# Numerators of two attention groups kept in SBUF, mixing factors formed and transposed earlier in a visit, and head 0 of a recurrence tied behind three sums

## The chip, the cores and the metric

The kernel runs on one core of a Trainium2 chip. The metric is the device time of one execution in microseconds, as the median of several runs. TensorE is PE in the profile, VectorE is DVE, ScalarE is ACT, GpSimd is POOL and SyncE is SP. Matrix products write into PSUM banks, of which there are eight; DVE and ACT read them from there. DMA transfers are issued by SP, POOL and ACT.

## The reference

One layer of an encoder for 1024 positions of width 1024, in float32:

```python
proj = x @ w_in          # aq, ak, av: 12 heads x 64; gq, gk: 4 x 64; gv: 4 x 128; gates
for gi, (win, dil) in enumerate(((128, 1), (512, 4), (2048, 16))):   # three groups of 4 heads
    o_g, lse_g = dilated_group(aq, ak, av, bias(gi), dil, win // 2 // dil)
mix_w = softmax(stack(lses), axis=0)
y_attn = sum(mix_w * stack(outs))                       # 1024 x 256
o_gla = gla_forward(...) + flip(gla_backward(...))      # decays by chunk, 4 heads
y_gla = o_gla * rsqrt(mean(o_gla ** 2)) * gla_norm_g * silu(gout)
merged = sigmoid(gate_a) * (y_attn @ wa) + sigmoid(gate_g) * (y_gla @ wg)
x = layernorm(ALPHA * x + merged @ w_out)
x = layernorm(ALPHA * x + square(relu(x @ w_ff1 + b)) @ w_ff2 + b)
```

A query attends keys within a window of its group, at a stride; each group has its own softmax, and the three outputs are mixed with weights that follow from the three softmax denominators. With e = exp(score − m) and den = sum(e) of a group, the mixed output is the sum over groups of exp(m_g − M)·(e_g·v) divided by the sum of exp(m_g − M)·den_g, M being the largest of the three m_g. The kernel calls e_g·v the numerator and exp(m_g − M) divided by that sum the factor.

## The kernel before

A product of two float32 matrices is made of three matmuls on parts: every operand is split into a rounded high part (a copy or cast on ACT) and a remainder (a subtraction on DVE), and `mm3` (L99 to L104) issues high·high, high·low and low·high. The large projections use seven products of half-size blocks in place of eight (Winograd's form of Strassen's scheme), so sums of blocks are formed on DVE ahead of the matmuls and sums of products behind them (`add`, L160). Twelve matmuls of 128x512 are called a step here.

**The order.** A scheduler decides the order of instructions on each engine from its own estimate of time; `tc.issue_after(x)` forbids it to put an instruction ahead of x, and `behind("name")` is that with the last instruction recorded under the name. The dictionary `issued` holds these: "add" is the last sum of products, "pe" the last matmul of a projection or of the recurrence, "small" the last small matmul of attention, "raw" and "sp" the last transfer issued on SP, "pool" the last one on POOL. All engines work in their own order and wait for others by semaphores.

**Head 0 of the recurrence.** At the end of the first projections (`psteps`, ten steps, L724 to L743) PE makes the products of q and k for the recurrence. Each step's result is read by a sum on DVE into `fu` or `fcr` and stored to `spill` in DRAM; the banks are called mm, tr and av. While that goes on, head 0 is prepared: `pre1` makes logarithms of decays, `scan` (L513, L514) sums them by chunk, `pre2` (L520 to L533) subtracts, makes exponentials on ACT, and multiplies k by `ex` and q by `zb` on DVE. `load_qk` brings q and k of heads 0 and 1 back from `spill` by SP: two transfers for each. The pieces `firsts[p]` belong to the next projections: `[0]` issues the load of weights `raw`, `[1]` casts them to `whi` on ACT (L93) and makes `wlo` on DVE (L95). Behind the steps follow `fill(1)` (two steps of the next projections, copied out by ACT at L630 as `xb`), `turn` (transposes k, ACT copies `kt`, L542), `intra` (scores inside a chunk, L581) and `kv` (k transposed times v, L550).

**Attention.** 24 tiles of 128 queries, in the order of group 2, group 1, group 0 (g = 2, 1, 0, eight tiles t each), are worked off between the steps of the projections of gates. `visit(i)` is issued at step `at[i]` and holds parts of several tiles: the loads of tile i+1, the value products of tile i−2 (L941, into the bank `avp`), the scores of tile i (L902, into two banks sc; DVE adds the bias and takes the row minimum, L908, and ACT makes the exponentials), the mixing of tile i−2, the transposes of the exponentials of tile i−1 (L926, into two banks tr; DVE and ACT copy them to `et`), and `spread` of tile i−1. A step later follow `weigh`, `shares`, `loadw` and `store`. For groups 2 and 1 the numerator is copied from `avp` to SBUF (L954), stored to `numdr` in DRAM by POOL, and brought back later by SP in quarters (`quarter`) into the tiles R. For group 0, `weigh` and `shares` (L986 to L1002) form the factors f from the minima and denominators of the three groups, `spread` transposes f on PE (L1008) into the score bank of the newest scores, ACT copies that to `fT` and stores it to `fdr`, `loadw` reads it back, repeated over 64 partitions, into W, and `mix` multiplies numerators by W and adds (L962 to L971). The result goes to `yadr`.

**The gates.** `gate_load` and `gate` bring the outputs of the recurrence and their gates into SBUF, apply silu on ACT, multiply and split on DVE, at fixed steps of the same loop.

The rows at which the profile points are these lines: L102 to L104 matmuls, L160 sums, L95 and L93 splits of weights, L530 and L533 the products with k and q, L542 and L550 `kt` and `kv`, L902, L908, L926, L941, L954, L962, L970, L1002 and L1008 as above.

## Time and profile before

| | |
|---|---|
| median of 3 runs | 1371.03 us (1369.74 to 1373.22) |
| the profiled execution | 1369.64 us, span 1367.9 us, clock of TensorE 0.996 |
| first projections, head 0 | to about 110 us of the span |
| recurrence, with first products of the next projections | 110 to about 340 us |
| attention between projections | 341 us (first value product) to 566 us (last mixing) |
| merge, output projection, norms, feed-forward part | behind about 600 us |
| busy, share of the span | PE 98%, DVE 76%, ACT 47%, POOL 10% |

The waits view names, for an engine and a line, what it waited for, the sum in us, how often, and the longest. A row of a timeline has its start, its duration, the engine, the line, the operation with what it writes and reads, and in brackets how long the engine was idle before it and what ended that. A row of the windows view has the stretch, its length, then the busy time and number of instructions of PE, of PE's weight loads, DVE, ACT and POOL, then the clock that TensorE was granted (1.00 is full), the mean share of the 16 DMA engines, and GB/s.

### The profile page before, as it was taken

To read this page: it belongs to the slowest core of one execution; us is meant where nothing else is said; L and a number is where in the kernel's file an instruction comes from. 1 tells how busy PE (TensorE), PEld (TensorE's weight loads), DVE (VectorE), ACT (ScalarE), POOL (GpSimd) and SP (SyncE) were. 2 spreads that over 40 slices of the span, in tenths; PEclk is the share of its full clock that TensorE was granted. 3 is DMA by queue.
4 is the path that set the end of the run, shared out by engine and by line. 5 is a ranking of instruction groups with operands and counts; after the bars stand their busy time and mean duration, and the time that the engine had idled before them with its cause. 6 is when DMAs were issued, how large, how long until landed. Compare 5 with 4: busy or idle time off the path is not lost.

```text
span 1367.9 us, 19100 instructions
## 1 busy us (share of the span) xinstructions
PE 1346.4 (98%) x6757; PEld 1119.6 (82%) x6757; DVE 1033.7 (76%) x1786; ACT 637.6 (47%) x1200; POOL 143.5 (10%) x228
## 2 busy tenths in 40 slices
PE   9989999999999998999999999999999999999998
PEld 8968898898877776788888888888888888888886
DVE  7767674576787897766667777877867897786988
ACT  7436674322456443345326655554556433333333
POOL 0001232101435333100001000000000000000002
PEclk9999999999999999999999999999999999999999
DMA  8386565775676777565835466656745955444313
GB/s 316 135 251 204 184 210 170 268 225 192 225 233 211 229 225 196 178 211 183 326 147 190 162 223 201 222 203 206 242 189 160 378 203 167 154 134 160 104 35 124
DMA packets 129700, 272.71 MB, mean 199 GB/s; under 512 B 36677, under 2 KB 48293, under 8 KB 129092
## 3 DMA queue, kind: packets, MB, share of 16 engines
q1 hardware_dynamic: 114004, 233.02, 51.3%
q0 software_dynamic: 12032, 36.97, 8.4%
q10 hardware_dynamic: 3568, 1.49, 0.4%
q8 instruction: 53, 0.87, 0.3%
q14 instruction: 43, 0.35, 0.1%
HBM read 185.57 MB, written 89.01 MB: 201 GB/s over the span
## 4 chain that ended last, share of the span: by engine, by line
PE 59%; DVE 1%; ACT 1%; DMA 1%; issue 0%; POOL 0%; ACTq 0%; DVEq 0%; POOLq 0%
PE ps L102 18%; PE ps L103 18%; PE ps L104 18%; PE mm L102 1%; PE mm L103 1%; PE mm L104 1%; ACT xr L1417 1%; DMA W<-fdr 0%; PE ps L1414 0%; DMA fdr<-fT 0%; PE ps L1925 0%; DVE cr L160 0%; DVE W L970 0%; PE ps L1921 0%; ACT T L1398 0%
## 5 line engine op out<-in xcount | busy, mean ns | idle before, releaser
L1398 ACT CAST T<-hp 128x1024 fp32r<-128x1024 f32 x36 | 37.9, 1052 | 109.8 <-PE ps L103 70.3
L1904 POOL TENSOR_TENSOR mv<-mv,mhalf 128x1 f32<-128x1 f32 x8 | 7.0, 878 | 607.3 <-DVE mv L1903 605.8
L103 PE MATMUL ps<-B,B 128*128 128x512 f32 x160 | 62.2, 389 | 0.0
L104 PE MATMUL ps<-B,B 128*128 128x512 f32 x160 | 62.2, 389 | 0.0
L102 PE MATMUL ps<-B,B 128*128 128x512 f32 x160 | 60.9, 390 | 0.5 <-ACT B L1398 0.5
L914 ACT ACTIVATE e<-e,sm 128x256 f32<-128x256 f32 (+2 forms) x96 | 43.3, 453 | 33.5 <-DVE sm L908 33.3
L102 PE MATMUL ps<-T,T 128*128 128x512 f32 x144 | 56.0, 389 | 0.0
L103 PE MATMUL ps<-T,T 128*128 128x512 f32 x144 | 56.0, 389 | 0.0
L104 PE MATMUL ps<-T,T 128*128 128x512 f32 x144 | 56.0, 389 | 0.0
L102 PE MATMUL ps<-B,T 128*128 128x512 f32 x144 | 56.0, 389 | 0.0
L103 PE MATMUL ps<-B,T 128*128 128x512 f32 x144 | 56.0, 389 | 0.0
L104 PE MATMUL ps<-B,T 128*128 128x512 f32 x144 | 56.0, 389 | 0.0
L1399 DVE TENSOR_TENSOR T<-hp,T 128x1024 fp32r<-128x1024 f32 x36 | 44.0, 1222 | 15.2 <-ACT T L1398 15.1
L1799 DVE TENSOR_TENSOR acc<-ps,acc 128x512 f32<-128x512 f32 x68 | 45.7, 688 | 12.7 <-PE ps L104 12.2
L102 PE MATMUL mm<-xB,whi 128*128 128x512 f32 x128 | 51.0, 398 | 0.0
L102 PE MATMUL ps<-T,fraw 128*128 128x512 f32 x128 | 49.6, 390 | 0.4 <-ACT T L1398 0.4
L103 PE MATMUL mm<-xB,whi 128*128 128x512 f32 x128 | 50.0, 390 | 0.0
L104 PE MATMUL mm<-xB,wlo 128*128 128x512 f32 x128 | 50.0, 390 | 0.0
L103 PE MATMUL ps<-T,fraw 128*128 128x512 f32 x128 | 49.8, 389 | 0.0
L104 PE MATMUL ps<-T,fraw 128*128 128x512 f32 x128 | 49.6, 389 | 0.0
L160 DVE TENSOR_TENSOR cr<-cu,mm 128x512 f32<-128x512 f32 x45 | 34.4, 767 | 18.7 <-PE mm L104 18.4
L1398 ACT CAST B<-hp 128x1024 fp32r<-128x1024 f32 x20 | 21.0, 1052 | 55.4 <-PE ps L103 48.1
(742 smaller groups left out, 4336.4 us busy)
## 6 DMA issues: line engine op xcount, KB each, us to landing
hdr<-c SPq DMA_DIRECT2D x112, 256.0 KB, 2.7
hp<-hdr SPq DMA_DIRECT2D x56, 512.0 KB, 3.8
spill<-cr SPq DMA_DIRECT2D x48, 256.0 KB, 3.6
raw<-in_wfm SPq DMA_DIRECT2D x17, 512.0 KB, 4.5
praw<-in_wfm SPq DMA_DIRECT2D x16, 512.0 KB, 6.4
pwhi<-in_wfm SPq DMA_DIRECT2D x16, 512.0 KB, 5.2
gate<-spill SPq DMA_DIRECT2D x32, 256.0 KB, 4.1
wa<-in_w SPq DMA_DIRECT2D x16, 512.0 KB, 4.6
```

Source lines behind the costliest of these rows:

```text
L102: T.matmul(ps, lh, rh, start=first and i == 0, stop=False, skip_group_check=more)
L103: T.matmul(ps, lh, rl, start=False, stop=False, skip_group_check=more)
L104: issued["pe"] = T.matmul(ps, ll, rh, start=False, stop=last and i == n - 1, skip_group_check=more)
L160: issued["add"] = V.tensor_tensor(o, a, b, op=OP.add)
L914: issued["exp"] = A.activation(e, e, AF.Exp, bias=sm[:, h:h + 1], scale=-1.0, accum_out=sm[:, 4 + h:5 + h])
L1398: A.copy(o[:, 0], src)
L1399: V.tensor_tensor(o[:, 1], src, o[:, 0].bitcast(F32), op=OP.subtract)
L1417: A.activation(q[i][:, k], tp[:, k], AF.Identity, bias=cols[:, c + 8:c + 9], scale=cols[:, c:c + 1])
L1799: V.tensor_tensor(m, p, m, op=OP.add)
L1904: G.tensor_tensor(mv[:, 3:4], mv[:, 2:3], mhalf[:, 0:1], op=OP.pow)
```

## The change

**Head 0.** `load_qk` issues k ahead of q. The scans stand at steps 4 and 6 in place of 4 and 5, and `pre2`'s subtraction behind the second scan. The two products on DVE (and the exponential of `zb` on ACT) become a function `scaled`, which head 0 calls behind the ten steps, "behind add", so behind the last sum; heads 1 to 3 call it where the code stood. The split of `firsts[1]` is tied behind the last sum issued at that point, and that of `firsts[2]` behind the scaling of q.

```diff
@@ scan, pre2, scaled
+                issued["scan"] = V.tensor_tensor_scan(L[64:128, rs], rm[64:128, rs], zb[64:128, rs], 0.0, OP.mult, OP.add)
...
-            V.tensor_tensor(Xc, Lc, Lc[:, :, 64:65].to_broadcast([128, 8, 128]), op=OP.subtract)
+            with behind("scan"):
+                V.tensor_tensor(Xc, Lc, Lc[:, :, 64:65].to_broadcast([128, 8, 128]), op=OP.subtract)
...
-            V.tensor_tensor(qk["k", h], qk["k", h], ex, op=OP.mult)
+            st["ex"] = ex
+            if h:
+                scaled()
+
+        def scaled():
+            zb = st["zb"]
+            with behind("add"):
+                issued["kx"] = V.tensor_tensor(qk["k", h], qk["k", h], st["ex"], op=OP.mult)
             with tc.issue_after(issued.get("ss", issued["pe"]).ins):
                 issued["zb"] = A.activation(zb, zb, AF.Exp, scale=1.0 / TAU)
-            V.scalar_tensor_tensor(qk["q", h], qk["q", h], 0.125, zb, op0=OP.mult, op1=OP.mult)
+            with tc.issue_after(issued["kx"].ins):
+                issued["qx"] = V.scalar_tensor_tensor(qk["q", h], qk["q", h], 0.125, zb, op0=OP.mult, op1=OP.mult)
@@ the ten steps
-        if n in (4, 5):
-            heads[0]["scan"](n - 4)
+        if n in (4, 6):
+            heads[0]["scan"](n // 2 - 2)
         if n == 6:
             heads[0]["pre2"]()
         if n == 7:
-            with tc.issue_after(issued["zb"].ins):
+            with behind("add"):
                 firsts[1][1]()
             firsts[3][0]()
             issued["sp"] = issued["raw"]
+    heads[0]["scaled"]()
```

On DVE around head 0 (fu and fcr are the sums, tr and av the banks they read, `wlo` the split of weights), before:

```order
L513 SCALAR_TENSOR_TENSOR L<-rmask,zb 64x512
L514 SCALAR_TENSOR_TENSOR L<-rmask,zb 64x512
L520 TENSOR_TENSOR zb<-L 128x1024
L160 TENSOR_TENSOR fcr_116<-fu_115,tr 128x512
L530 TENSOR_TENSOR k_984<-k_984,ex 128x1024
L160 TENSOR_TENSOR fcr_116<-fcr_116,av 128x512
L533 SCALAR_TENSOR_TENSOR q_981<-q_981,zb 128x1024
L95 TENSOR_TENSOR wlo<-raw,whi 128x1024
L160 TENSOR_TENSOR fcr_117<-fu_115,tr 128x512
L95 TENSOR_TENSOR wlo<-raw,whi 128x1024
L160 TENSOR_TENSOR fcr_118<-fu_115,av 128x512
```

and now (the lines of the changed kernel, L159 is the same sum, L537 and L541 are k and q):

```order
L159 TENSOR_TENSOR fcr_115<-fu_114,tr 128x512
L512 SCALAR_TENSOR_TENSOR L<-rmask,zb 64x512
L513 SCALAR_TENSOR_TENSOR L<-rmask,zb 64x512
L520 TENSOR_TENSOR zb<-L 128x1024
L159 TENSOR_TENSOR fcr_115<-fcr_115,av 128x512
L95 TENSOR_TENSOR wlo<-raw,whi 128x1024
L159 TENSOR_TENSOR fcr_116<-fu_114,tr 128x512
L159 TENSOR_TENSOR fcr_117<-fu_114,av 128x512
L537 TENSOR_TENSOR k_980<-k_980,ex 128x1024
L541 SCALAR_TENSOR_TENSOR q_983<-q_983,zb 128x1024
L95 TENSOR_TENSOR wlo<-raw,whi 128x1024 x2
```

The first sum stands ahead of the second pair of scans, and the products with k and q stand behind all sums. On ACT the casts of the second and third pair of weights, the two copies `xb` and the two copies `kt` keep their places.

**Attention.** The numerators of groups 1 and 2 go straight from `avp` into a tile N of SBUF (128 x 2 x 2 x 1024), so `numdr`, the 16 stores and the 16 loads of `quarter` are gone. Two tiles of group 1 with the same keys share one load of k and one of v. In a visit, `spread` of tile i−1 now stands directly behind the value products and writes into the second bank tr (`trs[1]`); `weigh` and `shares` of tile i stand in the same visit directly behind its scores; the mixing of tile i−2 follows them. The mixing adds into W, without a tile of its own.

```diff
@@ visit
-        for n, part in ((i + 1, 0), (i - 2, 3), (i, 1), (i - 2, 8), (i - 1, 2), (i - 1, 6)):
-            if 0 <= n < 24:
+        for n, part in ((i + 1, 0), (i - 2, 3), (i - 1, 6), (i, 1), (i, 4), (i, 5), (i - 2, 8), (i - 1, 2)):
+            if 0 <= n < 24 and (i != 16 or part not in (4, 5)):
                 tiles[n][part]()
-        if i in (12, 16):
+        if i in (12, 15):
             stats(2 if i == 12 else 1)
@@ the parts are load 0, scores 1, turned 2, values 3, weigh 4, shares 5, spread 6, loadw 7, mix 8, store 9
-                tp = issued["sps"][0][0:12, 0, 0:128]
+                tp = trs[1][0:12, 0, 0:128]
...
-                with tc.issue_after(issued["add"].ins):
+                with behind("biased"):
                     V.tensor_tensor(den, den, f[:, 0], op=OP.mult)
...
-                issued["shared"] = V.tensor_tensor(f[:, 0:3], f[:, 0:3], f[:, 4:5].to_broadcast([128, 3, 4]), op=OP.mult)
+                issued["add"] = issued["shared"] = V.tensor_tensor(f[:, 0:3], f[:, 0:3], f[:, 4:5].to_broadcast([128, 3, 4]), op=OP.mult)
...
             if g:
-                st = st_t()
-                V.tensor_copy(st, av)
-                pool_dma(numdr[g - 1, :, :, t * 128:t * 128 + 128].rearrange("b p n -> p b n"), st)
+                V.tensor_copy(N[:, g - 1, :, t * 128:t * 128 + 128], av)
@@ where the visits stand
-    at = [n0 + 2 + (i * 2.7 if i < 8 else 19 + (i - 7) * 1.8 if i < 16 else 35.2 + (i - 16) * 2.7) for i in range(26)]
+    at = [n0 + 2 + (i * 2.8 if i < 8 else 21.6 + (i - 8) * 1.8 if i < 16 else 36.2 + (i - 16) * 2.74) for i in range(26)]
...
-        for k, part, later in ((i, 4, 1), (i, 5, 1), (i - 1, 7, 1), (i - 2, 9, 1)):
+        if i == 16:
+            units[n + 1] = [tiles[i][4], tiles[i][5]]
+        for k, part, later in ((i - 1, 7, 1), (i - 2, 9, 1)):
```

On PE in a visit of group 0 (the sixth transpose of factors), before, where L941 are the values, L902 the scores, L926 the transposes of the exponentials (two banks) and L1008 the transpose of the factors:

```order
L941 MATMUL avp<-et_2458,av_2452 64x128
L941 MATMUL avp<-et_2459,av_2452 64x128
L902 MATMUL sc<-ak_2449,aq_2446 128x256 x4
L926 MATMUL tr<-ident,e_2455 128x128 x4
L926 MATMUL tr<-ident,e_2456 128x128 x4
L1008 MATMUL sc<-ident,f_2464 12x128
L102 MATMUL mm<-yT_2396,pwlo 128x512
```

and now, where L961, L922, L946 and L1027 are the same four:

```order
L961 MATMUL avp<-et_2459,av_2451 64x128
L1027 MATMUL tr<-ident,f_2464 12x128
L922 MATMUL sc<-ak_2449,aq_2446 128x256 x4
L946 MATMUL tr<-ident,e_2455 128x128 x4
L102 MATMUL mm<-yB_2396,pwhi 128x512
L103 MATMUL mm<-yB_2396,pwhi 128x512
L104 MATMUL mm<-yB_2396,pwhi 128x512
```

The transpose of the factors now stands ahead of the scores and in a bank tr. Of the transposes of the exponentials, those into the second bank follow nine matmuls of a projection later.

On DVE in the same visit, before, from the bias and minimum of the scores (L908) on:

```order
L908 ISA e_2454,sm_2461<-sc,strip_4147 128x256
L908 ISA sm_2461 128x1
L156 TENSOR_TENSOR pwlo<-psum_2408,pwlo 128x512
L962 TENSOR_TENSOR W<-avp,W 128x256
L970 TENSOR_TENSOR W<-R_2465,W 128x128 x4
L933 COPY et_2457<-tr 128x512
L986 TENSOR_TENSOR f_2463<-sm_2461,s_2467 128x4
```

and now (L980 is the first operation of the mixing, L953 the copy `et`, L1005 to L1021 the factors):

```order
L928 ISA e_2454,sm_2461<-sc,strip_4137 128x256
L928 ISA sm_2461 128x1
L953 COPY et_2457<-tr 128x512
L1005 TENSOR_TENSOR f_2463<-sm_2461,s_2465 128x4
L1006 TENSOR_TENSOR f_2463<-f_2463,s_2465 128x4
L1007 TENSOR_TENSOR f_2463<-f_2463,sm_2461 128x4
L1008 TENSOR_TENSOR f_2463<-f_2463,s_2465 128x8
L159 TENSOR_TENSOR cr_2404<-cu_2400,mm 128x512
L1015 TENSOR_TENSOR sm_2461<-sm_2461,f_2463 128x4
...
L1021 TENSOR_TENSOR f_2463<-f_2463 128x12
L980 TENSOR_TENSOR W<-avp,W 128x256
L988 TENSOR_TENSOR W<-N,W 128x128 x4
```

The mixing, which is what reads `avp`, stood right behind the scores and stands now behind the ten operations on f.

**The gates.** They are loaded in 16 transfers of 256 KB, two for each half of a head, at steps 32+7h+2q, and applied at steps 36+7h+2q; the splits of heads 2 and 3 move to the last two steps of the loop (`split`). The ring of tiles for split weights has six in place of seven tiles from step 21 on (before: step 30). The tiles of the pool "act" have tags of their own, so each takes the place of a named one.

```diff
+    def gate_load(h, q):
+        if h == q == 0:
+            assert all(t is not px for t in psides)
+            yg.append(cx.tile([128, 2, 512], F32, tag="px", name="pg"))
+            yg.append(xp.tile([128, 2, 4, 512], F32R, tag="act1", name="yg0"))
+        sl = slice(512 * q, 512 * q + 512)
+        pool_dma(yg[0][:, q], spill[4 + h, :, sl])
+        pool_dma(y2[:, h % 2, sl], yodr[h, :, sl])
+
+    def gate(h, q):
+        if q == 0:
+            A.activation(yg[0], yg[0], AF.Silu)
+        y = y2[:, h % 2, 512 * q:512 * q + 512]
+        with behind("add"):
+            V.tensor_tensor(y, y, yg[0][:, q], op=OP.mult)
+            if h < 2:
+                o = yg[1][:, :, 2 * h + q]
+                halve(o[:, 0], o[:, 1], y)
...
+        def split(n):
+            o = yg[1][:, :, n]
+            with tc.issue_after(issued["add"].ins):
+                halve(o[:, 0], o[:, 1], y2[:, n // 2, n % 2 * 512:n % 2 * 512 + 512])
```

More of the change, by code (lines that the diff above doesn't have):

```diff
@@ L478, in load_qk @@
         b, i = h // 2, h % 2
-        for nm, base in (("q", 0), ("k", 2)):
+        for nm, base in (("k", 2), ("q", 0)):
             qk[nm, h] = t = piece4(f"{nm}{h}")
@@ L610, in outt @@
             pool_dma(yodr[h, :, half * 512:half * 512 + 512], o)
-        return dict(pre1=pre1, scan=scan, pre2=pre2, turn=turn, kv=kv, states=states, intra=intra, out=out, outt=outt)
+        return dict(pre1=pre1, scan=scan, pre2=pre2, scaled=scaled, turn=turn, kv=kv, states=states, intra=intra, out=out, outt=outt)
     todo = []
@@ L693, in build, with behind_q @@
     extra = {}
+    def behind_q():
+        with behind("qx"):
+            firsts[2][1]()
     for p in range(2, NP):
         n = p if p < 8 else p + 4
-        extra.setdefault(n - 2, []).append(firsts[p][1])
+        extra.setdefault(n - 2, []).append(firsts[p][1] if n > 2 else behind_q)
     for p in range(4, NP):
@@ L866, in load @@
         def load():
-            b["q"], b["k"] = q, k = kq_t(), kk_t()
-            for o, base, c0, n in ((q, 24, t * 128, 128), (k, 30, k0, w)):
+            kn = 256 if g == 1 else w
+            first = g != 1 or t % 2 == 0
+            if first:
+                shared["k"] = kk_t()
+            b["q"], b["k"] = q, k = kq_t(), shared["k"]
+            for o, base, c0, n in ((q, 24, t * 128, 128), (k, 30, k0, kn))[:1 + first]:
                 pool_dma(o[:, :, 0:n], spill[base + 2 * g:base + 2 * g + 2, :, c0:c0 + n].rearrange("b p n -> p b n"))
@@ L896, in scores @@
             b["blks"] = blks
-            issued["sps"] = sps = [sc_t() for _ in range(2)]
+            sps = [sc_t() for _ in range(2)]
             for pr in range(2):
@@ L994, in shares @@
                 f, den, o = b["f"], b["sm"][:, 4:8], s12[:, t, :, 4:8]
-                with tc.issue_after(issued["add"].ins):
+                with behind("biased"):
                     V.tensor_tensor(den, den, f[:, 0], op=OP.mult)
-                with tc.issue_after(issued["add"].ins):
+                with behind("biased"):
                     V.tensor_tensor(o, o, f[:, 1:3], op=OP.mult)
@@ L1026, in stats @@
                                             smdr[g - 1, 512 * u:512 * u + 512].rearrange("(t p) w -> p t w", p=128))
-    def quarter(n):
-        u, q = n // 2, n % 2
-        for g in (1, 2):
-            c = ORD[g]
-            for pr in range(2):
-                src = numdr[g - 1, pr].rearrange("p (c u q j) -> p u q c j", c=c, u=2, q=2)[:, u, q]
-                dst = R[n % 2][:, g - 1, pr].rearrange("p (c j) -> p c j", c=c)
-                with behind("sp"):
-                    issued["sp"] = SP.dma_start(dst, src)
@@ L1060, in gate @@
-    def gate(hs, part):
-        if hs[0] % 2 == 0 and part == 0:
-            yg.append(xp.tile([128, 2, 4, 512], F32R, tag="act", name=f"yg{hs[0]}"))
-        if part == 0 and hs == (0, 1):
-            A.activation(yraw[0][:, :, 0], yraw[0][:, :, 0], AF.Silu)
-        elif part == 0:
-            for h, sl, t in gates[hs]:
-                A.activation(t[:, 0], t[:, 0], AF.Silu)
-        n = 2 if hs == (0, 1) else 1
-        h, sl, t = gates[hs][part // n]
-        q = part % n
-        g, y = (t[:, i, 512 * q:512 * q + 512] for i in range(2))
-        o = yg[h // 2][:, :, 2 * (h % 2) + sl.start // 512 + q]
+    yg = []
@@ L1386, in build @@
     XR = [xrp.tile([128, KT, 512], F32, name=f"xr{i}") for i in range(2)]
-    X = {nm: xp.tile([128, 2, 4, 512], F32R, tag="act", name=nm) for nm in ("B11", "B21")}
+    X = {nm: xp.tile([128, 2, 4, 512], F32R, tag=f"act{i}", name=nm) for i, nm in enumerate(("B11", "B21"))}
     def ln1(t):
```

78 lines of the change are left out of this document (31 added, 47 removed).

## The prediction

> **What bounds the kernel now.** I read the page's busy shares first, then the waits of TensorE, then windows of 20 us to see where those waits lie, and last the timelines of the two places where they are long.
>
> ```profile
> PE 1346.4 (98%) x6757; PEld 1119.6 (82%) x6757; DVE 1033.7 (76%) x1786; ACT 637.6 (47%) x1200; POOL 143.5 (10%) x228
> ...
> PE sc L1008 <- DVE sm L908: 5.3, 4, 3.8
> PE av L102 <- DVE fcr L160: 4.1, 1, 4.1
> PE sc L1008 <- DVE f L1002: 1.8, 1, 1.8
> PE sc L902 <- DMA ak<-spill: 1.7, 2, 1.3
> PE tr L102 <- DVE fcr L160: 1.5, 1, 1.5
> ```
>
> TensorE (PE) is busy for 98% of a span of 1367.9 us, so a part of the change pays only if it takes away PE idle time, PE work or time at a low clock. The waits view (us in total, times, longest) has five large rows, 14.4 us together, and all are at places that the change touches. The windows (span, then PE busy, PEld, DVE, ACT, POOL, then the granted clock and the DMA share) show a second cost beside two of them:
>
> ```profile
> 80.00:100.00 20.00, 14.39 (x59) 11.15 (x58) 14.30 (x15) 6.48 (x11) 0.76 (x1) 0.93 0.90 245
> 100.00:120.00 20.00, 20.00 (x103) 16.60 (x103) 11.63 (x23) 10.92 (x14) 1.51 (x4) 0.90 0.58 189
> ...
> 520.00:540.00 20.00, 16.23 (x84) 12.76 (x83) 16.86 (x56) 6.06 (x17) 7.62 (x12) 0.91 0.64 183
> 540.00:560.00 20.00, 17.77 (x114) 14.03 (x113) 16.21 (x48) 6.46 (x18) 2.90 (x6) 1.00 0.72 203
> ...
> 580.00:600.00 20.00, 20.00 (x90) 16.57 (x89) 11.94 (x18) 8.51 (x13) 0.00 (x0) 1.00 0.74 237
> ```
>
> The clock is 1.00 except around 100 us and around 530 us, where the two longest idles stand. The price of that is in PE's timeline.
>
> ```profile
> 91.18 0.50 PE L102 MATMUL tr<-xB,swlo 128*128 128x512 f32 x1 [1.51 <-DVE fcr L160]
> 98.34 0.79 PE L102 MATMUL av<-xB,swlo 128*128 128x512 f32 x1 [4.10 <-DVE fcr L160]
> 104.33 0.39 PE L104 MATMUL mm<-xB,wlo 128*128 128x512 f32 x1
> ...
> 111.41 2.05 PE L550 MATMUL tr<-gv,kt 128*128 128x128 f32 x16
> ...
> 523.73 1.09 PE L941 MATMUL avp<-et,av 128*64 128x128 f32 x16
> ...
> 525.82 1.09 PE L926 MATMUL tr<-ident,e 128*128 128x128 f32 x8
> 530.68 0.30 PE L1008 MATMUL sc<-ident,f 128*12 128x128 f32 x1 [3.77 <-DVE sm L908]
> 530.72 0.70 PE L102 MATMUL mm<-yT,pwlo 128*128 128x512 f32 x1
> 534.45 0.39 PE L102 MATMUL mm<-yT,pwlo 128*128 128x512 f32 x1
> ```
>
> Between 98.34 and 104.33 there are 14 starts, 0.43 us apart, where full speed gives 0.23 (rows further on): 5.99 us against 3.26, so 2.7 us lost. Between 530.72 and 534.45 there are 9: 3.73 against 2.09, so 1.6 us lost. Idle of 1.5 or 1.8 us was followed by no slow stretch. The total at stake is 14.4 + 4.3 = 18.7 us.
>
> **Part 1, head 0 of the recurrence: what it removes.** DVE works in order. Its rows, ACT's for the same time, and the issue of a weight load from SP's queue:
>
> ```profile
> 88.05 1.22 DVE L514 TENSOR_TENSOR_SCAN L<-rmask,zb 64x512 f32<-64x512 bf16 x1
> ...
> 90.45 0.68 DVE L160 TENSOR_TENSOR fcr<-fu,tr 128x512 f32<-128x512 f32 x1
> 96.46 1.23 DVE L530 TENSOR_TENSOR k<-k,ex 128x1024 f32<-128x1024 f32 x1 [5.34 <-DMA k<-spill]
> 97.60 0.68 DVE L160 TENSOR_TENSOR fcr<-fcr,av 128x512 f32<-128x512 f32 x1
> ...
> 99.34 1.22 DVE L95 TENSOR_TENSOR wlo<-raw,whi 128x1024 fp32r<-128x1024 f32 x1
> ...
> 104.22 0.68 DVE L160 TENSOR_TENSOR fcr<-fu,av 128x512 f32<-128x512 f32 x1
> ...
> 102.01 1.04 ACT L93 CAST whi<-raw 128x1024 fp32r<-128x1024 f32 x1 [7.89 <-DMA raw<-in_wfm]
> 105.08 1.05 ACT L93 CAST whi<-raw 128x1024 fp32r<-128x1024 f32 x1 [2.03 <-DMA raw<-in_wfm]
> 107.32 0.59 ACT L630 COPY xb<-mm 128x512 f32<-128x512 f32 x1 [1.19 <-DMA spill<-fcr]
> 109.56 0.59 ACT L630 COPY xb<-mm 128x512 f32<-128x512 f32 x1 [1.65 <-PE mm L104]
> 110.04 1.08 ACT L542 COPY kt<-tr 128x512 f32<-128x512 f32 x2
> ...
> 100.58 0.33 SPq L625 DMA_DIRECT2D raw<-in_wfm  x1
> ```
>
> The k·ex product waits 5.34 us for a load, and the sum that frees the `av` bank is queued behind it. The change issues k's loads ahead of q's, puts that product, and q's scaling behind it, after all three sums, and moves one pair of scans (1.2 us each) behind the first sum. The sum at 90.45 then comes two scans earlier, about 88.0, and PE's 1.51 us falls away; the sum at 97.60 needs only the matmuls and the pair of scans and ends by about 92.5, before PE comes to it. So 1.5 + 4.1 + 2.7 = 8.3 us go, and PE, which came to the product with `kt` at 111.41 without an idle, comes to it at 103.1.
>
> **What is late next.** The product with `kt` (L550, then `kv`) needs the copy of `kt`, and ACT is in order too: two casts of weights that wait for their loads, two copies `xb`, then `kt`. These loads were already what ACT waited for (7.89 and 2.03 us), and the change moves neither these rows of ACT nor their bytes. Bounds: if both land when they do now, the last cast ends at 106.1, two copies 0.5 apart follow, and kt is done about 107.7: PE idles 4.6 us, falls to half clock again (2.7 us), and of 8.3 us 1.0 is left. If the last load comes 4.6 us earlier, nothing is left to wait for and all 8.3 us stay: it is issued at 100.58, when the subtraction at 99.34 has freed its buffer, and that subtraction now stands right behind the second sum, some 6 us earlier. Below: a longer slow stretch than now could make it −1. The DMA share in this window is 0.90, so the engines have no room to bring a transfer much earlier by issuing it earlier; I take kt at 106.5 to 107, an idle of about 4 us with 2.2 us of slow clock behind it, and a gain of **2 us**.
>
> [...]
>
> **Part 2, attention.** In a visit before, the transpose of the factors `f` goes into the score bank that the visit has just filled, so PE stands until DVE has read those scores (L908).
>
> ```profile
> 519.46 0.42 DVE L962 TENSOR_TENSOR W<-avp,W 128x256 f32<-128x256 f32 x1 [2.91 <-DMA W<-fdr]
> 529.86 0.42 DVE L908 CUSTOM_DVE_ANT_0 e<-sc,strip 128x256 f32<-128x256 f32 x1
> 530.89 0.42 DVE L908 CUSTOM_DVE_ANT_0 e<-sc,strip 128x256 f32<-128x256 f32 x1
> 531.84 0.42 DVE L962 TENSOR_TENSOR W<-avp,W 128x256 f32<-128x256 f32 x1
> ...
> 506.59 0.28 PE L1008 MATMUL sc<-ident,f 128*12 128x128 f32 x1 [0.83 <-DVE sm L908]
> 515.34 0.48 PE L102 MATMUL mm<-xT,pwhi 128*128 128x512 f32 x1
> 515.66 0.40 PE L103 MATMUL mm<-xT,pwhi 128*128 128x512 f32 x1
> 515.89 0.40 PE L104 MATMUL mm<-xT,pwhi 128*128 128x512 f32 x1
> ```
>
> DVE stood 2.91 us at 519.46 for the weights W, which come back through DRAM from the transpose that PE had made at 506.59; it then ran without a gap and came to the scores only at 529.86, and PE had waited 3.77 us. After the change the transpose stands first in the visit, behind `values`, in a bank of its own turn (`trs[1]`), and the mixing comes behind the visit's own scores and shares. So the f transpose waits for nothing that this visit makes: 5.3 + 1.8 = 7.1 us of idle and 1.6 us of slow clock go, and W is asked for some 2 us earlier and used some 3 us later, so the 2.91 us of DVE go too.
>
> Given back: (a) the transposes of the weights `e` now stand in two pieces with nine matmuls between them. A change of form costs 0.32 instead of 0.23 us (515.34 to 515.66 to 515.89) going in and again coming out, 0.18 us in each of 8 visits, 1.4 us. (b) The bank `avp` is now read by the mixing only after the scores, the copy `et` and ten small operations on f with an exponential of ACT between them. From the first L908 that is 1.4 + 0.7 + 0.7 (one sum in between) + about 2 for the small ones + 0.7 for ACT, 5.5 us, where 529.86 to 531.84 was 2.0. `values` of the next visit writes `avp`. A visit with two steps lasts about 8.9 us (24 matmuls of 0.23, and from 523.73 to 526.9 some 3.2 us of attention), the scores are there 2 us into it, and 2 + 5.5 + 0.4 leaves 1.0 us; one with three steps leaves 3.8. DVE is busy 16.2 to 16.9 of 20 us in these windows, so it will be late by more than 1 us now and then. Bounds: 0, and 1.5 us in each of 8 visits, 12; I take **2 us**, as the long visits let DVE catch up. Net 8.7 − 1.4 − 2 = **5.3 us**.
>
> The two waits for `ak` (1.7 us) are in the visits of group 1, which the change spaces 0.8 step later and whose loads of k and v it shares between two tiles; I take **1.5**, bounds 0 and 1.7. The numerators kept in SBUF take away 16 stores and 16 loads of 128 KB off PE's path; the DMA share there is 0.64 to 0.72 and no row of PE's waits for them, so I cost them at nothing, covered by the matmuls (bound 0 to +1). The later gates and the four added splits at the end of the projections cost DVE and ACT about 4 us, near 590, where PE is busy 20.00 of 20 us and DVE 11.94; without that cover they would cost up to 4.
>
> **Sum.** 2 + 5.3 + 1.5 = 8.8 us off the profiled execution's 1369.64, so 1360.8; the median of the runs shown is 1.4 above that execution, so 1362.2. I say **1362**.
>
> **Rivals.**
> Full gain: head 0's loads come early enough and DVE keeps up, 8.3 + 8.7 − 1.4 + 1.7 = 17.3, so 1353.7. For it: the buffer of the last weights is free earlier. Against it: a DMA share of 0.90. Chance 0.17.
> The wait moves: head 0 gains 0 (PE waits at kv in place of at the sums) and attention gives back 6 us, mostly at `avp`: 0 + 1.3 + 1.5 = 2.8, so 1368. Chance 0.17.
> It does not do what it says: the scheduler's order keeps PE behind DVE, or the time saved is waited for behind it, where the first transfers of the next stage set the pace; 1371. Against it: outside the five rows PE is idle for 21.5 − 14.4 = 7.1 us in the whole span. Chance 0.06.
> Slower: DVE becomes the bound in the eight visits of group 0, because `avp` is held until the shares are formed. It decides when a visit's DVE block, 5.5 us from the scores plus what is queued ahead of them, exceeds a visit's 6.9 us behind its scores, that is when DVE enters late by 1 us or more each time. With 2.5 us idle in eight visits and three slow stretches of 1.6, 24.8 are paid against 8.7 + 2 + 1.5 − 1.4 = 10.8: 14 slower, 1385; with 1.8 us and no slow stretch 1375. For it: DVE's 16.9 of 20 us at 520. Against: part of that was the work piled up behind 2.91 us of idle. Chance 0.07.
> My forecast (gain 5 to 13) has 0.53.
>
> **How the numbers follow.** About 0.3% (4 us) is what a measurement of this kernel can tell from no change. Faster: the forecast and the full gain whole, and a third of "the wait moves", whose size spreads around the 4 us, 0.53 + 0.17 + 0.06 = 0.76. Same: the rest of that and the change without effect, 0.11 + 0.06 = 0.17. Slower 0.07. The forecast with its unknown costs is 1357 to 1367; the range reaches to both neighbours, 1353 to 1369, and leaves out about 0.18, mostly above.
>
> **What would show it.** Right: no wait of PE for `fcr`, PE's `L1008` (now a `tr` transpose) without idle, clock 1.00 from 520 to 540, PE idle before `kv` (tr<-gv,kt) of about 4 us with ACT's `kt` behind a cast that waits for raw. Wrong: kv without a wait (then 8 us there), or rows "PE avp <- DVE W" with more than 4 us in total (then attention gives back its gain), or a new wait behind 560.

## The result and the profile after

The changed kernel takes 1363.80 us (median of 6 runs, 1361.33 to 1366.27), the kernel before on the same chips 1373.57 us (6 runs, 1369.74 to 1375.24). The ratio is 0.9933 with a 95% interval of 0.9914 to 0.9952, so about 9.2 us less; the forecast was 8.8. The two profiled executions, on which the readings below rest, differ by 8.3 us (1369.64 and 1361.33). But the gain does not lie where the forecast had put all of it. PE's waits after (us in total, times, longest), from the waits view of the changed kernel:

```profile
PE tr L557 <- ACT kt L549: 5.4, 1, 5.4
PE zp L335 <- DVE mhalf L443: 1.2, 1, 1.2
PE ps L1928 <- ACT dg L1927: 1.0, 1, 1.0
PE mm L104 <- DVE pwhi L155: 0.8, 1, 0.8
PE avp L961 <- ACT et L951: 0.7, 1, 0.7
...
PE sc L922 <- DMA ak<-spill: 0.2, 1, 0.2
```

Of the five rows of 14.4 us none is left at its old size, and a new one of 5.4 us stands at head 0: the product with `kt`. The windows (span, busy time of PE, PEld, DVE, ACT, POOL, clock, DMA share, GB/s) show the same:

```profile
80.00:100.00 20.00, 20.00 (x89) 16.32 (x88) 16.14 (x17) 7.06 (x11) 1.06 (x2) 1.00 0.88 237
100.00:120.00 20.00, 14.65 (x80) 12.68 (x79) 11.91 (x23) 11.04 (x15) 1.50 (x4) 0.83 0.60 196
...
500.00:520.00 20.00, 20.00 (x126) 15.58 (x126) 19.20 (x66) 9.14 (x27) 6.09 (x9) 1.00 0.62 196
520.00:540.00 20.00, 20.00 (x125) 15.74 (x124) 19.63 (x61) 8.38 (x25) 7.57 (x12) 1.00 0.67 211
540.00:560.00 20.00, 19.23 (x112) 14.87 (x111) 15.75 (x40) 5.76 (x12) 3.57 (x6) 1.00 0.62 198
```

The idle of 5.6 us in the window from 80 us is gone, and 5.35 us stand in the next one, with a clock of 0.83 there. From 500 to 560 PE has no wait but one of 0.8 us, for `pwhi` near 551. In the two windows in which DVE is busy 19.2 and 19.6 of 20 us PE does not wait for it.

Since both programs have the same 5592 matmuls of projections (L102 to L104) in the same order, the start of the k-th in one can be set against that of the k-th in the other. I did so for every run, at five places where the small matmuls of attention and recurrence ahead of them are the same too. The table has how much each stage gained on the profiled execution of before (us; a minus is a loss). The stretches are named by the times of before.

| kernel | to 78 (start) | 78 to 135 (head 0) | 135 to 366 | 366 to 488 (group 1, begin of group 0) | 488 to 577 (group 0) | to the end |
|---|---|---|---|---|---|---|
| changed kernel | −0.53 | 1.36 | −0.02 | 0.64 | 6.85 | 8.29 |

The start has no edit in it and differs by up to 2.9 us between executions (e9_traffic below); in that of the changed kernel the starts of matmuls are 0.43 us apart from 5.66 to 6.94, where those of before are 0.23 apart. What is lost there can be made up at head 0, where PE waits for another engine in any case (e9_traffic loses 2.85 at the start, gains 1.95 at head 0 and still waits 5.3 us for `kt`). So the first two columns are to be read as a sum: 0.8 us here.

### The profile page after: what moved, and what is told of

Same layout as the page of the kernel before. It is cut to its first block, busy times and chain, and to the rows that moved or that the text cites. A ratio compares the mean times of both kernels' runs of the same rounds, so it can differ in the third digit from the quotient of the medians.

```text
span 1359.6 us, 19030 instructions
## 1 busy us (share of the span) xinstructions
PE 1345.5 (99%) x6757; PEld 1119.3 (82%) x6757; DVE 1034.7 (76%) x1786; ACT 640.5 (47%) x1201; POOL 127.8 (9%) x208
## 4 chain that ended last, share of the span: by engine, by line
PE 66%; ACT 1%; DVE 1%; issue 0%; DVEq 0%; ACTq 0%
PE ps L102 18%; PE ps L103 18%; PE ps L104 18%; PE mm L104 3%; PE mm L102 3%; PE mm L103 2%; PE avp L961 1%; PE sc L922 1%; PE tr L946 1%; ACT xr L1420 1%; PE ps L1417 0%; PE ps L1928 0%; PE ps L1924 0%; ACT T L1401 0%; DVE W L988 0%
## 5 line engine op out<-in xcount | busy, mean ns | idle before, releaser
L104 PE MATMUL ps<-B,B 128*128 128x512 f32 x160 | 62.2, 389 | 0.0
L102 PE MATMUL ps<-B,B 128*128 128x512 f32 x160 | 60.9, 390 | 0.5 <-ACT B L1401 0.5
L104 PE MATMUL ps<-B,T 128*128 128x512 f32 x144 | 56.0, 389 | 0.0
L102 PE MATMUL ps<-T,T 128*128 128x512 f32 x144 | 56.0, 389 | 0.0
L104 PE MATMUL ps<-T,T 128*128 128x512 f32 x144 | 56.0, 389 | 0.0
L102 PE MATMUL ps<-B,T 128*128 128x512 f32 x144 | 56.0, 389 | 0.0
L102 PE MATMUL mm<-xB,whi 128*128 128x512 f32 x128 | 50.8, 397 | 0.0
L102 PE MATMUL ps<-T,fraw 128*128 128x512 f32 x128 | 49.6, 390 | 0.4 <-ACT T L1401 0.4
L104 PE MATMUL mm<-xB,wlo 128*128 128x512 f32 x128 | 50.0, 390 | 0.0
L104 PE MATMUL ps<-T,fraw 128*128 128x512 f32 x128 | 49.7, 389 | 0.0
L1520 ACT ACTIVATE c<-c,cols 128x512 f32<-128x512 f32 x48 | 34.7, 725 | 30.2 <-DVE c L1581 13.8
```

The source lines that it names most:

```text
L102: T.matmul(ps, lh, rh, start=first and i == 0, stop=False, skip_group_check=more)
L104: issued["pe"] = T.matmul(ps, ll, rh, start=False, stop=last and i == n - 1, skip_group_check=more)
L1520: A.activation(q, src, AF.Relu, bias=cols[:, 2 * j + f:2 * j + f + 1])
```

## The experiments

Twelve kernels were run. The stages of each, as above:

| kernel | start | head 0 | sum of both | 135 to 366 | 366 to 488 | 488 to 577 | to the end | ratio to before (95%) |
|---|---|---|---|---|---|---|---|---|
| changed kernel | −0.53 | 1.36 | 0.83 | −0.02 | 0.64 | 6.85 | 8.29 | 0.9933 (0.9914 to 0.9952) |
| e1_head0 | −0.32 | 0.24 | −0.08 | −0.04 | −0.13 | −0.22 | −0.47 | 1.0002 (0.9989 to 1.0016) |
| e2_att | −0.73 | 0.37 | −0.36 | −0.06 | 0.59 | 6.40 | 6.55 | 0.9947 (0.9932 to 0.9962) |
| e3_qk1_late | −2.08 | 7.37 | 5.29 | −0.04 | 0.60 | 6.15 | 12.00 | 0.9914 (0.9893 to 0.9935) |
| e4_kt_first | −0.09 | −0.31 | −0.40 | −0.05 | 0.63 | 6.03 | 6.16 | 0.9950 (0.9934 to 0.9967) |
| e5_both | 0.01 | 5.92 | 5.93 | −0.04 | 0.54 | 6.00 | 12.36 | 0.9891 (0.9876 to 0.9907) |
| e6_spread | 0.04 | 0.47 | 0.51 | −0.04 | −1.37 | 2.68 | 1.75 | 0.9977 (0.9963 to 0.9990) |
| e7_mix | −0.11 | 0.76 | 0.65 | −0.05 | −0.04 | 5.87 | 6.35 | 0.9924 (0.9908 to 0.9940) |
| e9_traffic | −2.85 | 1.95 | −0.90 | −0.04 | 0.70 | 5.94 | 5.68 | 0.9925 (0.9907 to 0.9942) |
| e10_spacing | −0.11 | 0.56 | 0.45 | −0.06 | −10.15 | 4.72 | −5.01 | 1.0019 (1.0005 to 1.0033) |
| e12_own_kv | −0.55 | 1.28 | 0.73 | −0.07 | −3.87 | 6.15 | 2.52 | 0.9955 (0.9941 to 0.9970) |
| e13_am | −0.45 | 5.84 | 5.39 | −0.03 | 0.09 | 5.94 | 11.39 | 0.9905 (0.9884 to 0.9927) |
| e14_before_spaced | −0.01 | 0.61 | 0.60 | −0.05 | −0.24 | 4.66 | 4.96 | 0.9973 (0.9959 to 0.9987) |

The profiled execution is one of several and can stand some us off the median of its kernel (that of e14_before_spaced is the fastest of ten, 1366.20 with a median of 1370.03; that of e12_own_kv is among the slowest two of seven, 1368.51 with a median of 1365.51); the ratio tells how much a kernel gains, the stages tell where.

### The two parts apart

e1_head0 is the kernel before with the edits of the first diff (head 0) alone, e2_att the kernel before with all the others.

> The kernel before with the head-0 part of the change alone. Theory: the stall behind the loads of k only moves. PE loses its waits for fcr (5.6 us) and gets one for kt of 5 to 5.5 us in front of the product with kt, with a slow clock behind it; 1 us faster than before, ratio 0.999. Rival: the gain of the change sits here and attention's moves are neutral: 8 us faster, ratio 0.994.

> The kernel before with the attention part of the change alone (numerators in SBUF, order of the visits, spacing, gates). Theory: 7 to 8 us faster than before, ratio 0.9945, the waits for fcr at 91 and 98 us stay, no wait of the transpose of f. Rival (gain in head 0): ratio 1.000.

Measured: 1373.05 and 1364.05 us beside 1372.47. Head 0 alone gains nothing, attention alone gains 7.3 us (1372.47 x 0.0053). In the waits view of e1_head0 the old waits for `fcr` are gone and the one for `kt` is there, while those of attention are as before:

```profile
PE tr L558 <- ACT kt L550: 5.6, 1, 5.6
PE sc L1021 <- DVE sm L921: 5.6, 4, 4.1
```

The theory holds and its rival falls. The sum of start and head 0 in the table says the same without e1: the six kernels with the unaltered edit of head 0 (changed kernel, e1, e7, e9, e10, e12) have a mean of 0.3 us there, the three without it (e2, e6, e14) have 0.25.

### Why `kt` is late: ACT's order or the transfers

In the changed kernel PE is through the scores of the first half at 103.2 us and then stands; the rows are of PE's, ACT's, SP's and DVE's timelines:

```profile
102.07 1.16 PE L588 MATMUL sc<-q,k 64*128 64x128 f32 x16
108.58 3.78 PE L557 MATMUL tr<-gv,kt 128*128 128x128 f32 x16 [5.35 <-ACT kt L549]
112.02 1.08 PE L495 MATMUL sc<-lrt,wzr 96*128 96x512 f32 x2
...
102.91 1.04 ACT L93 CAST whi<-raw 128x1024 fp32r<-128x1024 f32 x1 [8.41 <-DMA raw<-in_wfm]
105.54 1.04 ACT L93 CAST whi<-raw 128x1024 fp32r<-128x1024 f32 x1 [1.58 <-DMA raw<-in_wfm]
106.97 1.07 ACT L637 COPY xb<-mm 128x512 f32<-128x512 f32 x2 [0.39 <-DMA spill<-fcr]
107.92 1.09 ACT L549 COPY kt<-tr 128x512 f32<-128x512 f32 x2
...
96.16 0.33 SPq L632 DMA_DIRECT2D raw<-in_wfm  x1
...
91.76 0.68 DVE L159 TENSOR_TENSOR fcr<-fcr,av 128x512 f32<-128x512 f32 x1
...
95.84 0.69 DVE L159 TENSOR_TENSOR fcr<-fu,av 128x512 f32<-128x512 f32 x1 [1.66 <-PE av L104]
```

The second load of weights was issued at 96.16, 4.4 us earlier than before (100.58), and its cast began at 105.54, 0.5 us later than before (105.08). Issued earlier behind the same loads, it landed no earlier. Three edits tell apart what holds `kt`:

```diff
e3_qk1_late: the loads of q and k of head 1 behind the weights
-            for h in range(2):
-                load_qk(h)
+            load_qk(0)
             firsts[2][0]()
...
     heads[0]["scaled"]()
     del issued["add"], issued["decay"]
     issued["raw"] = issued["sp"]
+    load_qk(1)
e4_kt_first: the casts behind kt
-            A.copy(kt, tp)
+            issued["kt"] = A.copy(kt, tp)
...
         step(H["turn"], 1)
+        if h == 0:
+            behind_kt(2)          # firsts[2][1]() behind "kt"
+            firsts[4][0]()
+            behind_kt(3)
e5_both: both
```

> The changed kernel with the four loads of q and k of head 1 (1 MB) issued behind the second weight load in place of ahead of the first. Theory (kt is late because the transfers ahead of it fill the DMA engines until 107 us): the weights and the last stores land about 4 us earlier, the wait for kt falls from 5.4 us to 1 to 2 us, no slow clock; 5 us faster than the changed kernel. Rival (kt is late because of its place in ACT's order behind two casts, whatever the transfers do): the wait stays above 4 us and the time the same.

> The changed kernel with the casts of the second and third pair of weights tied behind the copies kt on ACT; the two copies xb stay ahead of kt. Theory (transfers): the first xb waits for the stores spill<-fcr that landed at 106.9, so kt is copied at 107.9 as before and PE waits 5 us; within 1 us of the changed kernel. Rival (the casts hold kt): kt copied by 104, the wait at most 1.5 us, 5 us faster than the changed kernel.

> The changed kernel with both edits of the two runs before: q and k of head 1 loaded behind the weights, and the casts of the second and third pair of weights tied behind the copies kt. Theory: with the transfers out of the way ACT's order is what is left; the exponential that k waits for stands ahead of the casts again, the wait of PE for k (1.0 us) goes and the wait for kt stays under 1 us; 5 to 7 us faster than the changed kernel, ratio to before 0.988. Rival (transfers decide alone, the order on ACT adds nothing): as the run with late loads, 0.991.

e4_kt_first is no faster than the changed kernel (0.9950 beside 0.9933): with the casts out of the way the copy `xb` ahead of `kt` waits for the stores of the sums, and `kt` comes at the same time. ACT's timeline of e4_kt_first:

```profile
107.08 1.07 ACT L637 COPY xb<-mm 128x512 f32<-128x512 f32 x2 [13.00 <-DMA spill<-fcr]
108.03 1.09 ACT L549 COPY kt<-tr 128x512 f32<-128x512 f32 x2
```

In e3_qk1_late, with 1 MB fewer ahead of them, both kinds of transfer land earlier (the first cast begins at 99.59 in place of 102.91, and `xb` is copied at 104.45 without a wait for the stores, where it had waited until 106.97) and no wait for `kt` is left (PE's and ACT's timelines of that kernel):

```profile
103.83 1.09 PE L547 MATMUL tr<-ident,k 128*128 128x128 f32 x8 [1.03 <-DVE k L537]
...
106.06 2.05 PE L557 MATMUL tr<-gv,kt 128*128 128x128 f32 x16
...
99.59 1.05 ACT L93 CAST whi<-raw 128x1024 fp32r<-128x1024 f32 x1 [7.12 <-DMA raw<-in_wfm]
105.41 1.08 ACT L549 COPY kt<-tr 128x512 f32<-128x512 f32 x2
```

The edit takes bytes away and also lets SP issue the two loads of weights earlier, the first at 90.43 us in place of 93.55, the second at 95.15 in place of 96.16. The second load took 6.3 us from issue to landing (101.4), where it had taken 9.3 in the changed kernel (105.5). So 3 of its 4 us are a shorter time under way, with fewer bytes ahead of it. Of the first load's 3.3 us (the cast at 99.59 in place of 102.91) 3.1 are the earlier issue.

The kernel gains 0.0019 in the ratio on the changed kernel, 2.6 us, with intervals that overlap, and 4.5 us at head 0 by the stages (5.29 less 0.83); the expected 5 is at the upper end of this. The scheduler now had put a cast that waits for its load (99.59) ahead of the exponential that k needs, so PE waited 1.0 us for k. With both edits that goes, and the product with `kt` follows on the scores without a wait (PE's timeline of e5_both):

```profile
101.53 1.16 PE L588 MATMUL sc<-q,k 64*128 64x128 f32 x16
102.80 2.05 PE L557 MATMUL tr<-gv,kt 128*128 128x128 f32 x16
...
105.67 0.50 PE L495 MATMUL sc<-lrt,wzr 96*128 96x512 f32 x1 [0.81 <-ACT am L589]
...
107.26 0.50 PE L495 MATMUL sc<-lrt,wzr 96*128 96x512 f32 x1 [1.09 <-DVE am L590]
```

e5_both takes 1358.99 us, ratio 0.9891: 15 us faster than before and some 5.8 us (0.0042) faster than the changed kernel. The transfers were the cause: moving them takes the wait for `kt` away, moving the casts alone does not. With the transfers out of the way ACT's order is what removes the wait for k, but the interval of e5_both overlaps that of e3_qk1_late, so what the second edit is worth by itself (3 us by the ratios) is not shown.

e13_am moves the cast of the third pair of weights behind the masking of `am`, for the two waits of 0.8 and 1.1 us that e5_both has left:

```diff
-            behind_kt(3)
         step(H["intra"], 0)
+        if h == 0:
+            with behind("amc"), behind("am"):
+                firsts[3][1]()
```

> The changed kernel with late loads of q and k of head 1, the cast of the second pair of weights behind the copies kt, and that of the third pair behind the masking of am, so that PE's waits of 0.8 and 1.1 us for am go. Theory: 1 to 2 us faster than the version with both edits, ratio to before 0.988. Rival: the later cast is waited for by the next matmuls, which give the same 1 to 2 us back, 0.989.

1358.50 us, ratio 0.9905 with an interval of 0.9884 to 0.9927: the same as e5_both. Of the two waits for `am` one of 0.9 us is left, and a new one of 1.1 us for `am` stands at the first outputs, so the wait moves on; that it is given back is as the rival had it, though not by the cast. e5_both is the version to keep.

### Attention: which edit carries the gain

e6_spread is the kernel before with only the transpose of f moved:

```diff
-                tp = issued["sps"][0][0:12, 0, 0:128]
+                tp = trs[1][0:12, 0, 0:128]
...
-        for n, part in ((i + 1, 0), (i - 2, 3), (i, 1), (i - 2, 8), (i - 1, 2), (i - 1, 6)):
+        for n, part in ((i + 1, 0), (i - 2, 3), (i - 1, 6), (i, 1), (i - 2, 8), (i - 1, 2)):
```

> The kernel before with one move alone: the transpose of f stands behind the value products and writes into the second bank tr; weigh, shares, mixing, numerators and spacing as before. Theory (the wait for the score bank was the cost): the waits of the transpose of f go, 7.1 us and the slow stretch of 1.6 us, 1.4 us come back from the split transposes; 6 to 7 us faster than before, ratio 0.995. Rival (f is not ready that early without the shares in the same visit, or W then comes late): PE waits for f or the values wait for avp, under 3 us faster.

Ratio 0.9977, 3.2 us faster, at the edge of what the rival said. The wait for the score bank is gone and one for f itself has come, with a slow stretch behind it (starts 0.43 us apart from 550.45 to 553.44, 0.23 apart from 553.82 on; PE's and DVE's timelines of e6_spread):

```profile
549.39 0.27 PE L1009 MATMUL tr<-ident,f 128*12 128x128 f32 x1 [3.33 <-DVE f L1003]
...
547.03 0.69 DVE L216 TENSOR_TENSOR psum<-psum,praw 128x512 f32<-128x512 f32 x1
...
549.17 0.16 DVE L1003 TENSOR_TENSOR f<-f 128x12 f32<-128x12 f32 x1
```

The shares are formed a step later there and their small operations stand between the sums and splits of the projection on DVE. PE waits for f 4.6 us in all there; e10_spacing below, which forms them in the visit itself at the same spacing, waits 1.2 us. So forming them in the visit is, as far as these two show, what makes the earlier transpose possible with little waiting.

e10_spacing is the changed kernel with the old positions of the visits, e14_before_spaced the kernel before with the new ones:

```diff
-    at = [n0 + 2 + (i * 2.8 if i < 8 else 21.6 + (i - 8) * 1.8 if i < 16 else 36.2 + (i - 16) * 2.74) for i in range(26)]
+    at = [n0 + 2 + (i * 2.7 if i < 8 else 19 + (i - 7) * 1.8 if i < 16 else 35.2 + (i - 16) * 2.7) for i in range(26)]
```

> The changed kernel with the visits spaced as before (group 1 about 0.8 step earlier, group 0 about one step earlier). Theory (order and bank carry the gain of attention; the spacing is worth at most the waits for ak): 0 to 1.5 us slower than the changed kernel, with waits for ak of 1 to 1.7 us. Rival (the spacing is what lets DVE keep up): waits of PE for f, W or et of 3 us or more, 4 us slower.

> The kernel before with the new spacing of the visits alone. Theory (the spacing keeps group 1 behind the landing of its keys, the order inside a visit is what helps group 0): the waits for ak go (1.7 us), the waits of the transpose of f and the slow stretch behind them stay at 5 to 9 us; 1 to 2 us faster than before, ratio 0.999. Rival (the spacing carries the gain of attention by itself): 6 to 7 us faster, ratio 0.995.

e10_spacing is the surprise: 1375.20 us, ratio 1.0019, slower than before. The stages say where: group 0 still gains 4.7 us, and 10.2 us are lost in the stretch of group 1. PE's timeline of e10_spacing there:

```profile
397.26 1.65 PE L922 MATMUL sc<-ak,aq 64*128 64x192 f32 x8 [3.93 <-DMA ak<-spill]
...
439.26 0.43 PE L961 MATMUL avp<-et,av 128*64 128x128 f32 x2 [1.02 <-DVE et L953]
440.63 1.67 PE L961 MATMUL avp<-et,av 128*64 128x128 f32 x14 [0.94 <-ACT et L953]
```

The first tile of group 1 needs keys that a projection has only just stored. In this execution that store was issued at 387.8, the load of `ak` behind it at 394.1, after 5.5 us of waiting for the store, and it landed at 397.1, when PE had stood 3.9 us. Before, the load was issued at 391.9 and landed at 394.9, and PE waited 1.28 us. In the changed kernel it is issued at 392.0 and lands at 395.7, no earlier, but the visit comes later, so the wait is 0.2 us. Counted from PE's rows, 5.2 of the 10.2 us are more idle (3.9 us for `ak`, 2.0 for `et` and 1.2 for f here, 1.9 in all before), and 5.0 are slower matmuls, behind that idle and behind the two short ones for `et` (granted clock 0.92 from 380 to 400, 0.91 from 400 to 420 and from 440 to 460). Neither expectation had this size. From the issue of the store to that of the load behind it 6.3 us passed here, 5.2 in the changed kernel and 3.4 before. In e10_spacing POOL had issued two gate loads of 256 KB at 386.5 and 387.3, right ahead of this store; in the changed kernel they were issued at 384.8 and 385.6, and the kernel before has none there. Whether they hold the store up isn't shown.

e14_before_spaced gives the other half: the spacing alone gains 3.7 us by the ratio. The waits for `ak` are gone, and the transpose of f, which still stands last in the visit and still waits for the scores to be read, waits 2.0 us in place of 7.1 (waits view of e14_before_spaced):

```profile
PE av L102 <- DVE fcr L160: 3.8, 1, 3.8
PE sc L1008 <- DVE sm L908: 2.0, 5, 0.6
```

My theory had left 5 to 9 us there. At the old spacing, one visit (the scores at 524.75) had met a DVE that was 5.1 us behind; at the new one no visit of group 0 meets it more than 2.0 us behind. Why the queue on DVE falls better at these places isn't shown.

So in group 0 the moved transpose alone gains 2.7, the spacing alone 4.7, the order, the bank and the shares without the spacing 4.7, and all together 6.9: they remove the same waits by two ways and do not add up. (Each of these is one profiled execution.) In the stretch of group 1 the spacing is what keeps the change from a loss of 10 us.

e12_own_kv has the new spacing, but each tile of group 1 loads its own k and v again:

```diff
-            kn = 256 if g == 1 else w
-            first = g != 1 or t % 2 == 0
+            kn = w
+            first = True
...
-            if g != 1 or t % 2 == 0:
-                shared["v"] = kv_t()
+            if True:
+                shared["v"] = kv_t()
```

> The changed kernel with a load of k and of v for every tile of group 1, as before, in place of one for two tiles; the spacing stays. Theory (sharing is worth the waits for ak): PE waits for ak 1 to 1.7 us, 1 us slower than the changed kernel. Rival (the later spacing alone removed them): no such wait, the same time.

Ratio 0.9955, beside 0.9933: about 3 us slower by the ratios, whose intervals overlap, and 4.5 us in the stages from 366 to 488, read from an execution that is 3 us above the median of its kernel. There are two waits for `ak`, 1.4 us together, and one that I had not expected (PE's timeline of e12_own_kv):

```profile
427.06 0.43 PE L960 MATMUL avp<-et,av 128*64 128x128 f32 x2
429.56 1.52 PE L960 MATMUL avp<-et,av 128*64 128x128 f32 x14 [2.06 <-ACT et L950]
431.01 1.65 PE L921 MATMUL sc<-ak,aq 64*128 64x192 f32 x8
...
434.00 0.48 PE L102 MATMUL mm<-xT,pwhi 128*128 128x512 f32 x1
```

So without sharing the waits for keys are back, as the theory had it. The wait for `et` has another cause, which stands on ACT (ACT's timeline of e12_own_kv):

```profile
423.73 1.28 ACT L1063 ACT_TABLE_LOAD   x1 [3.17 <-DMA pg<-spill]
425.03 1.06 ACT L1063 ACTIVATE pg<-pg 128x1024 f32<-128x1024 f32 x1
426.11 1.28 ACT L933 ACT_TABLE_LOAD   x1
...
429.14 0.36 ACT L950 COPY et<-tr 128x256 f32<-128x256 f32 x1
```

ACT stands until a load of the gates has landed (423.7), and the silu of the gates (L1063) with two table loads goes ahead of the exponentials and of the copy `et`. In the changed kernel that load landed at 421.9, and its wait of 0.7 us for `et` stands behind the same silu; so do the two waits for `et` in e10_spacing (silu at 435.70). No run moves the silu, so it is not shown how much of the 4.5 us belongs to sharing, nor whether the k and v loads that came back are why the gates' load landed later.

### Two costs that were set at little or nothing

e7_mix puts the mixing ahead of weigh and shares, so `avp` is read earlier; e9_traffic puts the removed transfers back, as stores that nobody reads.

```diff
e7_mix
-(i - 1, 6), (i, 1), (i, 4), (i, 5), (i - 2, 8), (i - 1, 2)):
+(i - 1, 6), (i, 1), (i - 2, 8), (i, 4), (i, 5), (i - 1, 2)):
e9_traffic
                 V.tensor_copy(N[:, g - 1, :, t * 128:t * 128 + 128], av)
+                pool_dma(numdr[0, g - 1, :, :, t * 128:t * 128 + 128].rearrange("b p n -> p b n"),
+                         N[:, g - 1, :, t * 128:t * 128 + 128])
...
+    for i in (16, 18, 20, 22):        # four stores of 128 KB by SP at each, behind "sp"
+        units[int(at[i]) + 1].append(lambda i=i: again((i - 16) // 2))
```

> The changed kernel with the mixing of tile i-2 ahead of weigh and shares of tile i, so avp is read about 3 us earlier in a visit. Theory (avp held longer cost little, what was left waits for et and pwhi): within 1 us of the changed kernel. Rival (holding avp costs 2 us or more): 2 us faster.

> The changed kernel with the removed traffic put back: 16 stores of 128 KB of numerators by POOL behind the copies, and 16 transfers of 128 KB by SP at the old places of the quarters (as stores, not loads; nothing reads them). Theory (numerators in SBUF cost nothing and bring nothing by their traffic): within 1 us of the changed kernel. Rival (less traffic is what made weights, keys and W come in time): 3 us or more slower, waits for ak or W in PE's or DVE's rows.

Ratios 0.9924 and 0.9925, the same as the changed kernel within their intervals, which are wide enough to hide 2 us. The rows of PE say more: in none of the three kernels does PE wait for the mixing, and group 0 gains no more in these two (5.87 and 5.94) than in the changed kernel (6.85). So no cost of the longer hold on `avp` or of the traffic of the numerators is seen here. What the numerators in SBUF make possible (the freed tiles R and `mixed`, one order for all quarters) can't be read from these two.

## Why the prediction was right

The time (1363.8 for 1362), the side and the range were right. By the steps:

- **What bounds the kernel: right.** All five rows of PE's waits were touched and went, and nothing behind 577 us changed (8.30 us gained at 577, 8.29 at the end).
- **Head 0, what it removes: right in each number.** The sums end at 92.4 and 96.5, PE waits for none of them, and it comes to the product with `kt` at 103.2 (forecast 103.1). 8.2 us were freed.
- **Head 0, what is late next: the right wait, the wrong size.** The failed term is "I take kt at 106.5 to 107, an idle of about 4 us with 2.2 us of slow clock behind it, and a gain of 2 us". `kt` was copied at 107.92, the idle was 5.35 us, and the product with `kt` and the next two matmuls took 4.3 us (108.58 to 112.93) where before they took 2.4 (111.41 to 113.77), at a granted clock of 0.52 from 108.5 to 113. The 2.2 us of slow clock were my estimate and no run shows them: the kernel before has 2.7 us behind an idle of 4.10 and 1.6 behind one of 3.77, and here it was 2.0. The gain of this part is 0 (e1_head0: 1.0002, interval 0.9989 to 1.0016). PE began on the product with `kt` at 108.58, later than even my late bound (107.7). I had set the landing between "when they do now" and 4.6 us earlier, and had let the earlier issue count for something. It counted for nothing: 4.4 us earlier issued, 0.5 us later cast. The step also missed a second wait: the copy `xb` ahead of `kt` waits for the stores of the sums, until 106.97. So "if the last load comes 4.6 us earlier, nothing is left to wait for" was wrong: e4_kt_first takes the casts away from there, and `kt` comes at the same time. All these loads were issued by SP, and no run here moves one to another engine, so what that would do is not shown.
- **Attention, the removed waits: right in sum.** 7.1 us of idle and the slow stretch of 1.6 us went. That the moved transpose "waits for nothing that this visit makes" was right for the whole change; e6_spread shows that the move without the shares waits 4.6 us for f.
- **Attention, given back: (a) and (b) too high.** Around the split-off piece of transposes only the way out costs more than a usual step: 0.32 us from 509.21 to 509.53 below, as forecast. The way in takes 0.23 us, like any other (508.63 to 508.86). From 488 to 577 the change gained 6.85 of 8.7. Counted from PE's rows, its idle there fell by 6.0 us, from 6.8 to 0.9 (0.8 of that the wait for `pwhi`), and its matmuls took 0.9 us less, where 1.6 us of slow clock had gone. So the new order costs about 0.7 us of matmul time, half of the 1.4 forecast for (a). For (b), `avp`, 2 us were taken and no row of PE waits for the mixing; e7_mix agrees. In the visits of the changed kernel at 507.5 and 527.9 us the mixing comes 4.7 us after the first L928, not 5.5. (The visit of two steps in that sum is 24 times 0.23 and 3.2, so 8.7 us and not 8.9; nothing hung on it.)

```profile
508.63 0.39 PE L104 MATMUL mm<-yB,pwlo 128*128 128x512 f32 x1
508.86 0.60 PE L946 MATMUL tr<-ident,e 128*128 128x128 f32 x4
509.21 0.48 PE L102 MATMUL mm<-yB,pwlo 128*128 128x512 f32 x1
509.53 0.40 PE L103 MATMUL mm<-yB,pwlo 128*128 128x512 f32 x1
509.76 0.40 PE L104 MATMUL mm<-yB,pwlo 128*128 128x512 f32 x1
```

- **The waits for `ak`: right place, too high.** 1.5 was taken; they went from 1.7 to 0.2, but the stretch gained 0.6, since a wait of 0.7 us for `et` came and PE's matmuls there took 0.4 us more. That wait stands behind the silu of the gates on ACT, whose move the prediction had priced only near 590 us, at nothing. What the step did not see is how much hangs on the spacing: without it the same change loses 10 us there (e10_spacing).
- **The numerators at nothing: right as far as seen** (e9_traffic).

The sum was close by luck, because misses cancel: in the profiled execution head 0 gave 1.2 us less than taken (by e1_head0 2 less) and the stretch of group 1 0.9 less, while group 0 gave 1.6 more (6.85 for 5.3). Of the rivals, "the wait moves" was true of head 0 and false of attention; "DVE becomes the bound" did not come, though DVE was busy 19.6 of 20 us.

## What to carry to other kernels

When a stall of an in-order engine is taken away, follow PE to its next operand and ask what that waits for: here the operand needed a copy that stood behind loads and stores, and most of the freed 8.2 us was waited for again there (5.35 us of idle and about 2 us of slow clock). Where the DMA engines had a busy share of 0.88 (80 to 100 us; 0.98 from 96.16 to 105.5, while the load was under way), one load issued 4.4 us earlier behind the same loads came no earlier (its cast began at 105.54 in place of 105.08); issuing 1 MB of other loads behind the weights instead was worth about 4.5 us at that place. And where small work is placed between large steps by a table, test the table apart from the order: here the same reordering gained 9 us with one spacing and lost 3 us with the other.
